# Attention scores from 16-bit pairs of turned heads in layer 0, and more buffers for raw weights

## The chip, the cores and the metric

The kernel runs on one core of one Trainium2 chip. The metric is the device time of one execution in microseconds (us). The kernel before takes 1107.42 us, the median of three runs (1106.44 to 1108.69).

A core has five engines, each with an instruction queue that it works off in order: TensorE (PE in the profile; its weight loads are listed apart as PEld), VectorE (DVE), ScalarE (ACT), GpSimd (POOL) and SyncE (SP). SP computes nothing here and only issues DMA transfers: loads of weights from HBM, and the DMA transposes that turn probability tiles. Tiles lie in SBUF. Matmul results lie in PSUM.

## The reference, cut to what matters

Two layers of a trunk run on 512 latent and 256 context tokens of width 1024. In each layer one input projection feeds two attentions: A, a neighbourhood attention of 8 heads, and B, a grouped-query attention of 8 query heads over 2 key heads, each head 64 wide. The change touches how q and k of B get from the projection to the scores.

```python
qb = _rope_2d(_rmsnorm(hs(b_q, GQA_Q_HEADS), q_norm_b), pos_row, pos_col)
kb = _rope_2d(_rmsnorm(hs(b_k, GQA_KV_HEADS), k_norm_b), pos_row, pos_col)
k_all = jnp.concatenate([ckb, kb], axis=1)
b_att = _gqa_latent(qb, k_all, v_all)
...
def _attend(q, k, v):
    s = jnp.einsum('bqkgd,btkd->bkgqt', q, k).astype(jnp.float32) * (HEAD_DIM ** -0.5)
    p = jax.nn.softmax(s, axis=-1).astype(v.dtype)
    return jnp.einsum('bkgqt,btkd->bqkgd', p, v)
...
o_a = (a_att * jax.nn.silu(a_z)) @ w_o_a
o_b = (b_att * jax.nn.silu(b_z)) @ w_o_b
merged = jax.nn.sigmoid(g_a) * o_a + jax.nn.sigmoid(g_b) * o_b
```

In layer 0 the context queries attend too (context keys only). Layer 1 needs latent queries alone.

## The kernel before

**Splitting.** To keep fp32 accuracy, a value is split into a high part (rounded) and a low part (the rest), and a product is a sum of matmuls over the parts. A weight tile arrives as `raw` (128x512, fp32); ACT casts it to `whi` (L405, L420), and DVE or POOL subtracts to get `wlo` (L408, L422). `raw_tile` gives these tiles out of three buffers in turn, so the DMA of a fourth waits in SP's queue until the subtraction of the first is done. There are eight `whi` and eight `wlo` buffers.

**Stages.** Each layer runs: projections of k, v and q of A; the neighbourhood attention (in layer 0 at about 150 to 300 us); projections of k, v and q of B (300 to 375 us), with rotary turns; the grouped-query attention (375 to 540 us); the merge. While an attention runs, PE also works through filler: pieces of the gate projections and of A's output projection, chunks of 24 matmuls (L435 to L437), placed between the heads. The two attentions each open a pool of tiles with `open_att` (tile width 512 for A, 768 for B).

**Order.** The program lists the operations; a scheduler that simulates the engines then sets each engine's order, so that moving one operation can reorder others. `behind` ties some to their place: the dot products of the modulation (L297: `rawb` times a broadcast row, on DVE) keep the order of the program on DVE.

**q and k of B.** `rope_heads` normalises and rotates a token tile; `turn` transposes it on PE into a PSUM tile `pst` (L529), and ACT copies that to `qb` (128 x 4 x 128, fp32) or `kb` (L543). After all tiles, `stage_k` makes, for each of the two key heads, `kh` (the high part on both halves of the partitions) and `kl` (the low part), with one DVE cast, two ACT casts and one POOL subtraction (L872 to L876). In the attention, `gq_first` calls `stage_q` for each of the eight heads: an ACT cast of 64x768 (L883) puts the high part of q on one half of the partitions, a DVE subtraction (L884) the low part on the other. So one matmul of the stacked q with `kh` and one with `kl` gives the score (L890, L891), 512 and 256 columns for each block of 128 queries.

**One head** of B in layer 0: for each of four query blocks PE writes a score tile `pss` (two buffers); DVE takes the row maxima (L1161); ACT takes the exponential and its sum (L1162), after which PE may use the buffer again; ACT rounds to 16 bits (`h`, L841), DVE or POOL subtracts the low part (L842), and SP issues the DMA transpose (L846). Then the context queries: L903 (maxima), L905 (a scalar added to them) on DVE, L909 (exponential) on ACT. The values of the head before follow: PE turns the reciprocals `r` (L851 on DVE, L853 on PE), multiplies the transposed probabilities (L1178, L1179; L925 for the context), ACT and DVE collect the result (`ho`, L828, L829), and POOL multiplies it into `zb` (L833). Once, `prepare` splits A's gated output into `gah` (ACT) and `gal` (POOL, four subtractions of 128x768, L672).

Of the kernel before, what the change touches and what calls it, by code (L numbers as in the profile page):

```python
# [28 lines left out]
NP_GQ = (2, 4)  # L29
NH_GQ = (3, 4)  # L30
# [4 lines left out]
P_UP = 2.0 ** 14  # L35
SPLIT_POOL = (1, 3)
# [36 lines left out]
def hybrid_kernel(es: ExitStack, tc, x, ctx, cvec, w_ada, w_ada0, small, gvec, w_in, w_o_a, w_o_b, w_out,  # L73
# [56 lines left out]
    cd = drp.tile([16, 128], F32, name="cd")  # L130
    gs = [drp.tile([128, 4, NTOK], F32, name=f"gs{c}") for c in range(4)]
# [40 lines left out]

    def raw_tile():
        return wp.tile([128, 512], F32, tag="raw", name=nm("raw"), bufs=3)
# [12 lines left out]
    G.memset(ehalf, -0.5)  # L187
# [39 lines left out]


# [295 lines left out]
    def turn(y, npair, dst, t, perm, g):  # L524
# [5 lines left out]
        if perm and t in (0, 3):  # L530

            src = pt.rearrange("p (j s n) -> p j s n", j=npair, s=2)
            d = dst[:, :, 0:512].rearrange("p j (s n) -> p j s n", n=64)
            if t == 0:
                d = d[:, :, 0:3:2, :]
            else:
                src, d = src[:, :, ::-1, :], d[:, :, 1:8:6, :]
        else:
            c0 = 128 * t + (64 if perm and t < 4 else 0)
            src = pt.rearrange("p (j n) -> p j n", j=npair)  # L540
            d = dst[:, :, c0:c0 + 128]
        if g is None:
            S.copy(d, src)  # L543
        else:
            S.activation(d, src, AF.Copy, scale=g)
# [49 lines left out]
    def layer(l, hx, nxt, start):  # L595
# [114 lines left out]
        kav = big("ka").rearrange("p (j n) -> p j n", j=4)  # L710
        if first:
# [7 lines left out]
            def evac_ak(ts):  # L719
# [9 lines left out]
                for i, t in enumerate(ts):  # L729
                    mul_heads(ys[t], ys[t], ss[:, 8 * i:8 * i + 8], 8)  # L730
                    to_channels(ys[t], 4, kav, t, False, gk)
# [3 lines left out]
        else:  # L735
# [3 lines left out]
            for t in range(6):  # L739
                tok_proj(w, 512, a_hx, t, evac_na(kav, False, gk, 4))  # L740
# [19 lines left out]
        w = load_w(W, C_AV, 512, KT, mix_lo)  # L760
        for t in range(6):
            tok_proj(w, 512, a_hx, t, evac_va)
            if first:
# [6 lines left out]
        qav = big("qa").rearrange("p (j n) -> p j n", j=4)  # L770
        w = load_w(W, C_AQ, 512, KT, mix_lo, own=hp["p"])
        za = big("za")
# [6 lines left out]
        for t in range(qt):  # L779
            tok_proj(w, 512, a_hx, t, evac_na(qav, True, gq, YB if first else 4))  # L780
# [10 lines left out]
        if True:  # L791
# [68 lines left out]
            def k_tile(e, zero):  # L860
                kh = att["p"].tile([128, 768], F32R, tag=f"kh{e}", name=nm("kh"), bufs=1)
                kl = att["p"].tile([128, 768], F32R, tag=f"kl{e}", name=nm("kl"), bufs=1)
                if zero:
                    V.tensor_scalar(rows(kl, 1 - e).rearrange("p (a b) -> p a b", b=128),
                                    rows(ident, 1 - e).unsqueeze(1).to_broadcast([64, 6, 128]),
# [664 lines left out]
```

## Time and profile before

| what | us |
|---|---|
| median of three runs (lowest, highest) | 1107.42 (1106.44, 1108.69) |
| profiled execution, its time | 1111.07 |
| span in that execution, first to last instruction | 1109.3 |
| PE busy in the span | 1075.5 |
| DVE busy | 767.4 |
| ACT busy | 617.1 |
| POOL busy | 473.1 |
| mean granted TensorE clock | 0.991 |

Busy time counts instructions in flight. Matmuls are pipelined, so that a row of the timeline shows a matmul of 0.4 us where the next one starts 0.23 us later; the step from start to start is what a matmul costs. "Idle before" in brackets is the time that an engine stood still ahead of an instruction, and the name behind the arrow is what ended the wait. PEclk is the share of full TensorE clock that was granted. The prediction shows the rows.

### The profile page before, as it was taken

Reading aid. Unit: us, or ns where it says so; the run is one execution under the profiler, and the core shown is the slowest. Engines: PE = TensorE matmul, PEld = TensorE weight load, DVE = VectorE, ACT = ScalarE, POOL = GpSimd, SP = SyncE. Lnnn points to the kernel's source line nnn. Section 1 sums busy time; section 2 is a strip of 40 time slices with the busy share of each in tenths; the row PEclk is TensorE's granted clock in tenths of the full one; section 3 lists DMA queues with packets and bytes.
Section 4 is the critical chain, followed back from the end, with each engine's and each line's share of the span. In section 5 each row is a group of like instructions: output and inputs, shape, how many; then the busy total and the mean of one; then the engine's idle time right before and its main releaser. Section 6 shows DMA issues by size and latency. Waiting matters only on the chain. (4 is left out here: it accounts for less than half of the span.)

```text
span 1109.3 us, 16937 instructions
## 1 busy us (share of the span) xinstructions
PE 1075.5 (97%) x5672; PEld 879.1 (79%) x5672; DVE 767.4 (69%) x1600; ACT 617.1 (56%) x1236; POOL 473.1 (43%) x397
## 2 busy tenths in 40 slices
PE   8999999999999989989999999999999999999998
PEld 5688888788888868767788878888877888777677
DVE  4667889975377487766777785366997665677473
ACT  6454279776433566765330275444899446786430
POOL 1054235555257154463621354232355472564531
PEclk9999999999999999998999999999999999999999
DMA  9455324554543379789633542453565536879642
GB/s 370 146 171 153 90 68 111 128 138 120 169 131 127 100 184 215 166 228 228 213 101 124 157 147 78 140 163 101 134 149 130 156 107 171 199 229 239 188 152 77
DMA packets 236000, 171.79 MB, mean 155 GB/s; under 512 B 160140, under 2 KB 201864, under 8 KB 234248
## 3 DMA queue, kind: packets, MB, share of 16 engines
q1 hardware_dynamic: 228576, 156.31, 51.6%
q0 software_dynamic: 2368, 7.87, 2.1%
q10 hardware_dynamic: 4968, 6.53, 1.8%
q8 instruction: 45, 0.74, 0.3%
q14 instruction: 43, 0.35, 0.1%
HBM read 115.58 MB, written 17.32 MB: 120 GB/s over the span
## 5 line engine op out<-in xcount | busy, mean ns | idle before, releaser
L842 POOL TENSOR_TENSOR h<-p,h 128x256 f16<-128x256 f32 (+2 forms) x104 | 113.6, 1101 | 160.0 <-ACT h L841 117.7
L422 POOL TENSOR_TENSOR wlo<-raw,whi 128x512 fp32r<-128x512 f32 x70 | 98.0, 1406 | 131.6 <-ACT whi L420 98.7
L435 PE MATMUL psf<-hx,whi 128*128 128x512 f32 (+1 forms) x360 | 138.2, 384 | 2.2 <-DVE zt L627 1.2
L436 PE MATMUL psf<-hx,whi 128*128 128x512 f32 (+1 forms) x360 | 136.1, 378 | 0.0
L437 PE MATMUL psf<-hx,wlo 128*128 128x512 f32 (+1 forms) x360 | 136.1, 378 | 0.0
L435 PE MATMUL psx<-whi,hx 128*128 128x512 f32 (+1 forms) x328 | 121.0, 372 | 0.0
L437 PE MATMUL psx<-whi,hx 128*128 128x512 f32 (+1 forms) x328 | 120.0, 367 | 0.0
L420 ACT CAST whi<-raw 128x512 fp32r<-128x512 f32 x136 | 83.2, 620 | 65.5 <-DMA raw<-in_w_in_dram 46.9
L436 PE MATMUL psx<-wlo,hx 128*128 128x512 f32 (+1 forms) x328 | 119.6, 366 | 0.0
L408 POOL TENSOR_TENSOR wlo<-raw,whi 128x512 fp32r<-128x512 f32 x40 | 59.8, 1499 | 117.7 <-ACT whi L405 74.6
L405 ACT CAST whi<-raw 128x512 fp32r<-128x512 f32 x88 | 54.3, 623 | 96.7 <-PE psx L437 34.2
L508 POOL TENSOR_TENSOR ss<-ss,ehalf 128x8 f32<-128x8 f32 (+2 forms) x40 | 63.6, 1593 | 77.2 <-DVE ss L505 72.2
L841 ACT CAST h<-p 128x256 f16<-128x256 f32 (+2 forms) x136 | 81.7, 616 | 5.3 <-DMA ht<-h 1.3
L422 DVE TENSOR_TENSOR wlo<-raw,whi 128x512 fp32r<-128x512 f32 x66 | 65.3, 992 | 25.9 <-ACT whi L420 24.3
L1161 DVE CUSTOM_DVE_ANT_0 p<-pss,vb 128x768 f32<-128x768 f32 x64 | 60.2, 953 | 31.0 <-PE pss L891 28.9
L1162 ACT ACTIVATE p<-pss,mx 128x768 f32<-128x768 f32 x64 | 57.6, 901 | 41.1 <-DVE mx L1161 40.4
L435 PEld LDWEIGHTS psf<-hx,whi 128*128 128x128 f32 x360 | 68.3, 190 | 14.9 <-ACT zt L625 1.9
L437 PEld LDWEIGHTS psf<-hx,wlo 128*128 128x128 f32 x360 | 68.2, 190 | 12.0
L436 PEld LDWEIGHTS psf<-hx,whi 128*128 128x128 f32 x360 | 68.3, 190 | 10.9
L437 PEld LDWEIGHTS psx<-whi,hx 128*128 128x128 f32 x328 | 61.9, 189 | 10.2
L436 PEld LDWEIGHTS psx<-wlo,hx 128*128 128x128 f32 x328 | 62.0, 189 | 9.5
L435 PEld LDWEIGHTS psx<-whi,hx 128*128 128x128 f32 x328 | 61.8, 189 | 9.1 <-issue 0.2
(338 smaller groups left out, 2984.7 us busy)
## 6 DMA issues: line engine op xcount, KB each, us to landing
raw<-in_w_in_dram SPq DMA_DIRECT2D x168, 256.0 KB, 3.0
rawb<-in_w_ada_dram SPq DMA_DIRECT2D x48, 256.0 KB, 2.8
raw<-in_w_out_dram SPq DMA_DIRECT2D x32, 256.0 KB, 2.9
tg<-gs SPq DMA_DIRECT2D x4, 1536.0 KB, 9.9
rawx<-in_w_ada_dram SPq DMA_DIRECT2D x4, 1024.0 KB, 10.3
rawy<-in_w_ada_dram SPq DMA_DIRECT2D x4, 1024.0 KB, 10.3
gs<-zt ACTq DMA_DIRECT2D x16, 256.0 KB, 2.6
raw<-in_w_o_a_dram SPq DMA_DIRECT2D x16, 256.0 KB, 3.1
```

The costliest lines, as they stand in the source:

```text
L405: S.copy(hi[:, :n], raw[:, :n])
L408: e.tensor_tensor(lo[:, :n], raw[:, :n], F(hi[:, :n]), ALU.subtract)
L420: S.copy(hi, raw)
L422: lo_eng(i).tensor_tensor(lo, raw, F(hi), ALU.subtract)
L435: T.matmul(ps, lhs[0], rhs[0], start=first, stop=False)
L436: T.matmul(ps, lhs[0], rhs[1], start=False, stop=False)
L437: T.matmul(ps, lhs[1], rhs[0], start=False, stop=last)
L508: G.tensor_tensor(ss, ss, ehalf[:, :n], ALU.pow)
L841: S.copy(h[:, 0], p[:, :n])
L842: eng.tensor_tensor(h[:, 1], p[:, :n], h[:, 0], ALU.subtract)
L1161: V.tensor_tensor_reduce(p, pss, lift, -1.0, 3e38, ALU.add, ALU.min, mx[:, 0:1])
L1162: S.activation(p, pss, AF.Exp, bias=mx[:, 0:1], accum_out=r[:, i:i + 1])
```

## The change

**Pairs in layer 0's grouped-query attention** (`GQ_PAIRS = (True, False)`). `turn` no longer copies the transposed tile as fp32. It writes fp16 pairs straight from PSUM: for q, ACT casts each half of the partitions (64 x 4 x 128) to the high part on its own half, and DVE subtracts the low part into the other half, so that `qb` holds the stacked q of every head, and `split_q` (the old `stage_q`) is not called. For k, one ACT cast and one DVE subtraction of 128x128 for each of six tiles, and then four DVE copies of 64x1536 (fp16) put each key head on both halves. To fit fp16, the norm gains are scaled by factors from their largest entries (`head_scales`, a few small operations at the stage's start), and the scores are scaled back by `gq_ndq` in L1161's place and `gq_dq` in the exponentials. The 160 score matmuls of this stage (64 of 512 columns, 96 of 256) take fp16 operands instead of fp32r.

**More raw buffers** (`MORE_RAW`). While an attention is open, every second `raw` tile comes from a second set: of one buffer in layer 0's neighbourhood attention and two in layer 1's, of three in layer 0's grouped-query attention, and none in layer 1's. The number of DMA transfers stays the same.

The same pairs for the neighbourhood attention are in the code and switched off (`NA_PAIRS`), so that none of their lines runs. Of the diff, what runs:

```diff
+MORE_RAW = ((1,2),(3,0))
+NA_PAIRS = (False, False)
+GQ_PAIRS = (True, False)
...
+H_UP = 2.0 ** 11
...
+    more_raw = {"p": None, "n": 0}
     def raw_tile():
-        return wp.tile([128, 512], F32, tag="raw", name=nm("raw"), bufs=3)
+        n = 3
+        if more_raw["p"] is not None:
+            more_raw["n"] += 1
+            if more_raw["n"] % 2 == 0:
+                return more_raw["p"]()
+        return wp.tile([128, 512], F32, tag="raw", name=nm("raw"), bufs=n)
...
-    G.memset(ehalf, -0.5)
+    G.memset(ehalf[:, 0:24], -0.5)
...
+    def head_scales(rows, inv, up):
+        S.activation(rows, rows, AF.Abs)
+        V.tensor_reduce(inv, rows, AX, ALU.max)
+        V.tensor_scalar(inv, inv, G_MIN, 1.0 / H_UP, ALU.max, ALU.mult)
+        V.reciprocal(up, inv)
...
+        def pair(hi, lo, x, g):
+            if g is None:
+                S.copy(hi, x)
+                todo.append(lambda: V.tensor_tensor(lo, x, hi, ALU.subtract))
...
+        kind, a, b = dst
+        for n0, n1, c0 in cuts:
+            x = pt.rearrange("p (j n) -> p j n", j=npair)[:, :, n0:n1]
+            da, db = [d[:, :, c0:c0 + n1 - n0] for d in (a, b)]
+            if kind == "k":
+                pair(da, db, x, g)
+                continue
+            for e, d in enumerate((da, db)):
+                own, other = slice(64 * e, 64 * e + 64), slice(64 - 64 * e, 128 - 64 * e)
+                pair(d[own], d[other], x[own], None if g is None else g[own])
+        run(todo, len(todo))
...
+            def stage_k(src, j, e, to, eng):
+                for half in range(2):
+                    eng(rows(to, half), rows(src, e)[:, :, j, :])
+            def q_pair(src, e, j):
+                return src[:, e, j, :]
...
+                pool, n_raw = att["p"], MORE_RAW[width == 768][l]
+                if n_raw:
+                    more_raw["p"] = lambda: pool.tile([128, 512], F32, tag="rawp", name=nm("raw"), bufs=n_raw)
+                st.callback(lambda: more_raw.update(p=None))
...
+                S.copy(g_abs, gbc)
+                head_scales(g_abs, g_inv, g_up)
+                V.tensor_scalar(gbc[:, 0, :], gbc[:, 0, :], g_up[:, 0:1], None, ALU.mult)
+                V.tensor_scalar(gbc[:, 1, :], gbc[:, 1, :], g_up[:, 1:2], 8.0, ALU.mult, ALU.mult)
+                V.tensor_tensor(gq_dq, g_inv[:, 0:1], g_inv[:, 1:2], ALU.mult)
+                V.tensor_scalar(gq_ndq, gq_dq, -1.0, None, ALU.mult)
...
-                    V.tensor_tensor_reduce(p, pss, lift, -1.0, 3e38, ALU.add, ALU.min, mx[:, 0:1])
-                    S.activation(p, pss, AF.Exp, bias=mx[:, 0:1], accum_out=r[:, i:i + 1])
+                    V.tensor_tensor_reduce(p, pss, lift, gq_ndq if gq_pairs else -1.0, 3e38, ALU.add, ALU.min, mx[:, 0:1])
+                    S.activation(p, pss, AF.Exp, bias=mx[:, 0:1], scale=gq_dq if gq_pairs else 1.0,
+                                 accum_out=r[:, i:i + 1])
...
-                q = stage_q(qbv[:, h // 2, :], h % 2)
+                kh, kl = gkt[h // 4][:2]
+                q = q_pair(qbv, h % 2, h // 2) if gq_pairs else split_q(qbv[:, h // 2, :], h % 2)
```

**Three places of the order.** Row by row: the line in the program, the operation, output<-inputs with buffer numbers, and the output's shape. In the program with the change the line of an operation is another: L297 is now L333, L422 L458, L829 L911, L842 L924, L851 L933, L854 L936, L903 L992, L905 L995, L1161 L1290, L417 L453, L846 L928, L953 L1051, L955 L1053.

First, DVE in the second head of layer 0's grouped-query attention, from the result of the head before (`ho`) to the first score of the next head. Before:

```order
L829 TENSOR_TENSOR ho_4525<-pst_4512,ho_4525 64x512
L903 TENSOR_REDUCE mx_4494<-pss_4489 128x2
L842 TENSOR_TENSOR h_4467<-p_4463,h_4467 128x768
L297 ISA rawb_4455,asum<-rawb_4455,vb_3419 128x512
L297 ISA asum 128x1
L851 RECIPROCAL r_868_4427<-r_868_4427 128x4
L905 TENSOR_SCALAR mx_4494<-mx_4494 128x2
L884 TENSOR_TENSOR qs_4932<-qb_3734,qs_4932 64x768
L829 TENSOR_TENSOR ho_4538<-psv_4529,ho_4538 64x256
```

With the change:

```order
L924 TENSOR_TENSOR h_4493<-p_4489,h_4493 128x768
L333 ISA rawb_4481,asum<-rawb_4481,vb_3419 128x512
L333 ISA asum 128x1
L911 TENSOR_TENSOR ho_4551<-pst_4538,ho_4551 64x512
L992 TENSOR_REDUCE mx_4520<-pss_4515 128x2
L933 RECIPROCAL r_866_4453<-r_866_4453 128x4
L995 TENSOR_SCALAR mx_4520<-mx_4520,vb_3419 128x2
L1290 ISA p_4711,mx_4712<-pss_4706,vb_3419 128x768
```

The subtraction for `h` and the dot product on `rawb`, which stood behind `ho` and ahead of the reciprocals of `r`, now stand ahead of `ho`; the subtraction for `qs` is gone.

Second, DVE two heads later, between the maxima of the context queries and the scalar added to them. Before:

```order
L829 TENSOR_TENSOR ho_5047<-psv_5038,ho_5047 64x256
L903 TENSOR_REDUCE mx_5003<-pss_4998 128x2
L884 TENSOR_TENSOR qs_5364<-qb_3734,qs_5364 64x768
L851 RECIPROCAL r_975_4936<-r_975_4936 128x4
L905 TENSOR_SCALAR mx_5003<-mx_5003 128x2
```

With the change:

```order
L992 TENSOR_REDUCE mx_5023<-pss_5018 128x2
L911 TENSOR_TENSOR ho_5067<-psv_5058,ho_5067 64x256
L933 RECIPROCAL r_971_4956<-r_971_4956 128x4
L995 TENSOR_SCALAR mx_5023<-mx_5023,vb_3419 128x2
L933 RECIPROCAL r_5027<-r_5027 128x2
```

The subtraction for `qs` has left the gap between the two, and the small `ho` (64x256) has come into it.

Third, SP's queue at the start of layer 0's neighbourhood attention, where the loads of filler weights (`raw`) stand between those of the position bias (`bint`, `bedg`) and the first transposes. Before:

```order
L953 DMA bint_1469<-in_bias_int_dram 128x256
L955 DMA bedg_1470<-in_bias_edge_dram 64x128 x2
L417 DMA raw_1645<-in_w_in_dram 128x2x256
L417 DMA raw_2025<-in_w_in_dram 128x2x256
L955 DMA bedg_1470<-in_bias_edge_dram 64x128 x2
L417 DMA raw_2031<-in_w_in_dram 128x2x256
L417 DMA raw_2037<-in_w_in_dram 128x2x256
L846 DMA_TRANSPOSE ht_1475<-h_1504 128x4x64 x2
L846 DMA_TRANSPOSE ht_1475<-h_1520 128x4x128
```

With the change:

```order
L1051 DMA bint_1473<-in_bias_int_dram 128x256
L1053 DMA bedg_1474<-in_bias_edge_dram 64x128 x2
L453 DMA raw_1637<-in_w_in_dram 128x2x256
L453 DMA raw_2041<-in_w_in_dram 128x2x256
L453 DMA raw_1649<-in_w_in_dram 128x2x256
L1053 DMA bedg_1474<-in_bias_edge_dram 64x128 x2
L453 DMA raw_2302<-in_w_in_dram 128x2x256
L453 DMA raw_2035<-in_w_in_dram 128x2x256
L928 DMA_TRANSPOSE ht_1479<-h_1508 128x4x64 x2
L928 DMA_TRANSPOSE ht_1479<-h_1524 128x4x128
```

One load more stands ahead of the first transposes, and the loads no longer go in the order of their numbers: those from the three old buffers run ahead of those from the one new buffer.

More of the change, by code (lines that the diff above doesn't have):

```diff
@@ L130, in hybrid_kernel @@
     cd = drp.tile([16, 128], F32, name="cd")
+    b_int = [drp.tile([8, 128, 256], F32, name=f"b_int{i}") for i in range(2)]
+    b_edge = [drp.tile([8, 128, 128], F32, name=f"b_edge{i}") for i in range(2)]
     gs = [drp.tile([128, 4, NTOK], F32, name=f"gs{c}") for c in range(4)]
@@ new lines, in turn @@
+        todo = []
+        if not isinstance(dst, tuple):
+            if perm and t in (0, 3):
+                x = pt.rearrange("p (j s n) -> p j s n", j=npair, s=2)
+                d = dst[:, :, 0:512].rearrange("p j (s n) -> p j s n", n=64)
+                if t == 0:
+                    d = d[:, :, 0:3:2, :]
+                else:
+                    x, d = x[:, :, ::-1, :], d[:, :, 1:8:6, :]
+            else:
+                x = pt.rearrange("p (j n) -> p j n", j=npair)
+                d = dst[:, :, cuts[0][2]:cuts[0][2] + 128]
+            if g is None:
+                S.copy(d, x)
+            else:
+                S.activation(d, x, AF.Copy, scale=g)
+            return
@@ L1034, in pipeline @@
                 run(fill, len(fill))
[L1036 removed]
+            akt = None if na_pairs else [k_tile(e) for e in range(2)]
             def na_first(h):
                 j, e = h // 2, h % 2
[L1040 to L1042 removed]
+                if na_pairs:
+                    kk = att["p"].tile([128, 2, 768], F16, tag="kk", name=nm("kk"), bufs=3)
+                    kh, kl = kk[:, 0], kk[:, 1]
+                    stage_k(kav, j, e, kk, V.tensor_copy)
+                    q = q_pair(qav, e, j)
+                else:
+                    kh, kl = akt[e]
+                    split_k(kav[:, j, :], e, kh, kl, False)
+                    q = split_q(qav[:, j, :], e)
                 st = na_scores(h, q, kh, kl)
```

144 lines of the change are left out of this document (94 added, 50 removed).

## The prediction

> **What bounds the kernel now.** I read the page's busy times first, then a table by stages, then PE's waits in the worst stage, then the timeline around the two longest of them. The page:
>
> ```profile
> span 1109.3 us, 16937 instructions
> PE 1075.5 (97%) x5672; PEld 879.1 (79%) x5672; DVE 767.4 (69%) x1600; ACT 617.1 (56%) x1236; POOL 473.1 (43%) x397
> ```
>
> PE has work in flight for 97% of the span, so only three things can shorten the kernel: cheaper matmuls, fewer idle gaps of PE, or a fuller clock. The table by stages (columns: window, its length, then busy time and count of PE, PEld, DVE, ACT, POOL, granted clock, DMA share, GB/s) tells where the gaps are:
>
> ```profile
> 150.00:300.00 150.00, 146.69 (x898) 125.21 (x897) 111.37 (x301) 109.63 (x247) 71.99 (x76) 1.00 0.51 129
> 300.00:375.00 75.00, 75.00 (x435) 65.48 (x435) 48.46 (x98) 29.72 (x60) 36.29 (x28) 1.00 0.40 129
> 375.00:540.00 165.00, 153.14 (x845) 123.38 (x844) 116.43 (x206) 104.58 (x203) 79.69 (x54) 0.96 0.78 193
> 920.00:1050.00 130.00, 126.53 (x595) 95.77 (x594) 83.93 (x134) 86.95 (x155) 67.19 (x45) 1.00 0.84 211
> ```
>
> Layer 0's grouped-query attention (375 to 540) has 11.9 us without a matmul, and it is the only one of these with a lower clock. Its twin in layer 1 (920 to 1050) misses 3.5, layer 0's neighbourhood attention 3.3, the projections of q and k (300 to 375) nothing. In windows of 10 us the clock falls twice:
>
> ```profile
> 405.00:415.00 10.00, 7.14 (x39) 6.07 (x40) 9.94 (x13) 4.22 (x10) 7.33 (x5) 0.79 0.38 107
> 415.00:425.00 10.00, 10.00 (x43) 7.36 (x42) 5.48 (x14) 5.82 (x10) 2.52 (x2) 0.87 1.15 235
> 495.00:505.00 10.00, 6.58 (x28) 5.48 (x27) 6.70 (x10) 3.90 (x7) 7.91 (x6) 0.72 1.05 342
> 505.00:515.00 10.00, 9.49 (x51) 7.78 (x49) 5.43 (x12) 4.18 (x9) 2.24 (x3) 0.93 1.00 244
> ```
>
> The missing clock is 2.1 + 1.3 = 3.4 us the first time and 2.8 + 0.7 = 3.5 the second. So the stage holds 11.9 + 6.9 = 18.8 us that are not matmuls at full rate, and that is the most that smoother running there can give. The largest waits of PE, on its timeline:
>
> ```profile
> 411.53 0.69 PE L853 MATMUL pst<-ident,r 128*128 128x128 f32 x2 [2.86 <-DVE mx L905]
> 452.64 0.50 PE L890 MATMUL pss<-gk,qs 128*128 128x512 f32 x1 [1.31 <-ACT p L909]
> 500.22 0.79 PE L890 MATMUL pss<-gk,qs 128*128 128x512 f32 x1 [2.71 <-ACT p L1162]
> ```
>
> Each drop of the clock goes with one of the two long ones. Both begin with a DVE instruction that took several times its usual length while POOL was at work:
>
> ```profile
> 406.77 4.61 DVE L297 CUSTOM_DVE_ANT_0 rawb<-rawb,vb 128x512 f32<-128x512 f32 x1
> 405.46 2.55 POOL L833 TENSOR_TENSOR zb<-zb,ho 64x512 f32<-64x512 f32 x1 [4.01 <-DVE ho L829]
> 407.98 1.63 POOL L842 TENSOR_TENSOR h<-p,h 128x768 f16<-128x768 f32 x1
> 409.58 1.25 POOL L422 TENSOR_TENSOR wlo<-raw,whi 128x512 fp32r<-128x512 f32 x1
> 493.94 3.60 DVE L842 TENSOR_TENSOR h<-p,h 128x768 f16<-128x768 f32 x1 [0.32 <-ACT h L841]
> 489.54 7.18 POOL L672 TENSOR_TENSOR gal<-za,gah 128x768 fp32r<-128x768 f32 x4
> ```
>
> The dot product on `rawb` that starts at 406.77 ends at 411.38, 0.55 us after POOL's row of three is through (409.58 + 1.25). The reciprocals of `r` stood behind it on DVE, and PE waited for them. The second time `h` is held until POOL is through with `gal`, and the maxima, the exponential and PE's score buffer behind it come late.
>
> **The change part by part.**
>
> *The work that moves.* From the attention go six q subtractions on DVE and six casts on ACT; two of each were done before 375 us. Into the projection stage come operations for which the trace has near rows only:
>
> ```profile
> L884 DVE TENSOR_TENSOR qs<-qb,qs 64x768 fp32r<-64x768 f32 x6 | 7.4, 1227 | 0.7 <-ACT qs L883 0.5
> L883 ACT CAST qs<-qb 64x768 fp32r<-64x768 f32 x6 | 5.0, 828 | 0.3 <-PE pst L853 0.3
> L829 DVE TENSOR_TENSOR ho<-pst,ho 64x512 f32<-64x512 f32 x8 | 5.5, 687 | 5.0 <-ACT ho L828 5.0
> L591 DVE TENSOR_TENSOR rr<-rr,ry 128x128 f32<-128x128 f32 x4 | 1.2, 288 | 1.2 <-POOL ry L588 1.1
> L872 DVE CAST gk<-kb 64x768 fp32r<-64x768 f32 x2 | 1.1, 549 | 0.0
> L543 ACT COPY qb<-pst 128x512 f32<-128x512 f32 x6 | 3.5, 584 | 5.3 <-PE pst L529 5.1
> ```
>
> DVE gets 12 subtractions of 64x512 from PSUM (12 x 0.687 = 8.2), six of 128x128 (6 x 0.288 = 1.7), four copies of 64x1536 for two casts of 64x768 (between 4 x 0.549 and twice that, less 1.1: 1.1 to 3.3), and loses two q subtractions (about 1 each): 9.0 to 11.2 us net, with the head scales some eight tiny operations more. ACT's six copies become twelve casts, about +3.5, against fewer k and q casts. At most 48.5 + 11 + 1 = 61 of 75 us of DVE are then busy, under a PE that is never idle there. I cost this move at nothing. PE covers it: in the new order 59 matmuls stand between the last turned tile and the first score, over 7 us at 0.12 each, while the last tile needs two casts and two subtractions, 2 x 0.58 + 2 x 0.69 = 2.5 us. With that cover gone it would cost 2.5.
>
> *Cheaper score matmuls.* Steps from start to start:
>
> ```profile
> 486.70 0.40 PE L890 MATMUL pss<-gk,qs 128*128 128x512 f32 x1
> 486.93 0.40 PE L891 MATMUL pss<-gk,qs 128*128 128x512 f32 x1
> 487.17 0.28 PE L890 MATMUL pss<-gk,qs 128*128 128x256 f32 x1
> 487.29 0.28 PE L891 MATMUL pss<-gk,qs 128*128 128x256 f32 x1
> 490.08 0.38 PE L1178 MATMUL pst<-ht,vb 128*128 128x512 f16 x1 [0.93 <-DVE zb L854]
> 492.45 0.38 PE L1179 MATMUL pst<-ht,vb 128*128 128x512 f16 x1
> 403.10 0.61 PE L925 MATMUL psv<-vb 128*128 128x256 f16 x4
> ```
>
> The 512-column score takes 0.235 (487.17 less 486.70, halved); the fp16 value matmuls of 512 columns, twelve between the two rows, step by 2.37 / 11 = 0.215. For 256 columns it is 0.12 against (0.61 - 0.28) / 3 = 0.11. So 64 x 0.02 + 96 x 0.01 = 2.2 us at most; nothing, if it is the score's place and not its type that sets the step. I take 1.5, nearer the fp16 rows.
>
> *The stall at 411.* In the new order `h` and the dot product stand ahead of `ho` on DVE. POOL's `zb` of 405.46 waits for that `ho`, so the row of three POOL operations can no longer be under way when the dot product starts; and the reciprocals of `r` now follow `ho` and a reduction from PSUM. The 2.86 us wait goes, and with it the drop of the clock, 3.4: 6.3 us. If the same collision only moves to POOL's `h` that now stands ahead of `zb`, DVE loses at most that operation's 1.63 us, and the gain shrinks by it.
>
> [...] Here the clock fell by waits of 2.86 and 2.71, so I go by the trace.
>
> *The wait at 452.* These rows carry it:
>
> ```profile
> 448.29 0.67 DVE L903 TENSOR_REDUCE mx<-pss 128x2 f32<-128x512 f32 x1
> 448.99 1.00 DVE L884 TENSOR_TENSOR qs<-qb,qs 64x768 fp32r<-64x768 f32 x1
> 450.11 1.42 DVE L905 TENSOR_SCALAR mx<-mx 128x2 f32<-128x2 f32 x1
> 449.39 2.12 POOL L842 TENSOR_TENSOR h<-p,h 128x768 f16<-128x768 f32 x1 [0.22 <-ACT h L841]
> L829 DVE TENSOR_TENSOR ho<-psv,ho 64x256 f32<-64x256 f32 x7 | 2.9, 420 | 3.9 <-ACT ho L828 3.7
> ```
>
> The tiny L905 is held until POOL's `h` ends (449.39 + 2.12 = 451.51). Without the q subtraction it would come sooner, but the small `ho` that now stands there (0.42 us) puts it at about 449.4 (448.29 + 0.67 + 0.42), just when POOL's `h` starts. The gain is 1.3 or nothing; I take nothing.
>
> *More raw buffers.* In the grouped-query stage none of PE's waits ends on a raw load, so a deeper prefetch saves nothing by itself: 0. In layer 0's neighbourhood attention half of the loads now go through one buffer, so each of these waits for the load two before it, where it waited for the load three before. Bounds: no cost, as PE's largest waits there are not for weights, and the slower rival below.
>
> ```profile
> PE psf L435 <- DVE zt L627: 1.2, 1, 1.2
> PE psv L925 <- DVE ho L832: 1.1, 1, 1.1
> ```
>
> *New waits.* DVE and ACT together have 12.4 us less to do in the attention's 165 (7.4 + 5.0), but the order on every engine is new. Between nothing and one more episode like 411's (6.3). I take one wait of the stage's usual size, +1.3.
>
> **Sum:** -1.5 - 6.3 + 1.3 = -6.5 us. The profiled execution took 1111.07 us (the span and 1.8 around it), 0.3% above the median of 1107.42; the terms are differences, so I set them against the median: 1107.4 - 6.5 = **1101 us**.
>
> **The rivals.**
>
> *Both episodes go.* The relieved DVE reaches `h` before POOL's four `gal` start, so that the 2.71 wait at 500 and its 3.5 of clock go too, and no new wait comes: 1101 - 6.2 - 1.3 = 1093.5. For it: the stage loses 12 us of DVE and ACT work. Against it: the four `gal` are untouched and still stand one behind another, 7.18 us in which an `h` on DVE can be caught.
>
> *The stall only moves.* Another two-input operation of DVE meets another row of POOL work, as POOL's `h` and `zb` come in every head. The score's 1.5 is kept, and 1.3 of new wait comes: 1107. Against it: the stage in layer 1 runs the same mix on the same engines with 3.5 us idle and a full clock. [...]
>
> *Slower: the single new buffer blocks SP's queue.*
>
> ```profile
> SPq L417 <- POOL wlo L422: 14.2, 3, 12.5
> ```
>
> One raw load already held SP for 12.5 us in the neighbourhood attention, waiting for a POOL subtraction. With loads out of turn (the third load of the new order belongs to a later chunk), such a wait can come with transposes behind it that PE needs. PE has one chunk of filler to bridge it, 24 x 0.23 = 5.5 us, so 12.5 - 5.5 = 7.0 us of wait and a drop of the clock, 3.4: 1101 + 10.4 = 1111. It decides from a hold of over 5.5 us. Against it: the 12.5 of before cost PE nothing.
>
> **How the numbers follow.** Chances: forecast 0.48 (1097 to 1105), both go 0.15, it only moves 0.22, the slower rival or another new episode 0.15. About 0.2%, 2.2 us, is what a measurement of this kernel can tell from no change. Faster: 0.46 of the forecast, 0.15 and 0.03, together 0.64. Same: 0.02, 0.14 and 0.01, 0.17. Slower: 0.05 of a stall that moves and grows, and 0.14, 0.19. The range leaves out about a tenth on each side: from 1092, just below the case that both go, to 1111.
>
> **What would show it.** Right: no DVE operation over 3 us ahead of the second head's reciprocals, one drop of the clock in this stage instead of two, PE idle there near 9 us, fp16 scores of 512 columns stepping by 0.215. Wrong: two or more drops of the clock still in the stage; PE idle between 300 and 375 (the cover fails); waits of PE for `ht` or for `wlo` in the neighbourhood attentions, where SP stood long on a raw load.

## The result, and the profile after

The changed kernel takes 1114.53 us (median of 6 runs, 1112.86 to 1115.50) against 1108.31 for the kernel before beside it: a ratio of 1.0053, 95% interval 1.0037 to 1.0070. It is 6 us slower, where 6.5 less had been forecast. The page of the profile after (span, then busy time of each engine):

```profile
span 1111.9 us, 16941 instructions
PE 1076.6 (97%) x5672; PEld 866.9 (78%) x5672; DVE 770.3 (69%) x1618; ACT 615.0 (55%) x1232; POOL 466.3 (42%) x395
```

The table by stages of the kernel after, with the columns of the prediction (window, its length, busy time and count of PE, PEld, DVE, ACT and POOL, granted clock, DMA share, GB/s):

```profile
300.00:375.00 75.00, 74.63 (x431) 64.85 (x430) 57.03 (x124) 28.04 (x59) 33.68 (x26) 1.00 0.45 139
375.00:540.00 165.00, 153.00 (x860) 113.55 (x860) 115.02 (x205) 105.22 (x199) 82.91 (x57) 0.97 0.80 189
610.00:690.00 80.00, 76.24 (x357) 61.01 (x356) 58.75 (x109) 37.13 (x84) 35.19 (x39) 1.00 0.39 124
775.00:850.00 75.00, 72.72 (x369) 58.68 (x369) 71.78 (x200) 69.09 (x153) 39.45 (x41) 0.98 0.62 143
```

The same table of the kernel before, for the two stages of which the prediction shows no row:

```profile
610.00:690.00 80.00, 78.08 (x371) 64.12 (x370) 58.92 (x110) 39.42 (x87) 37.34 (x39) 1.00 0.40 125
775.00:850.00 75.00, 73.38 (x381) 58.87 (x380) 69.76 (x197) 68.46 (x152) 35.42 (x40) 1.00 0.58 139
```

Two stages that the prediction never priced are worse: layer 0's merge with layer 1's first projections (610 to 690) has 3.8 us without a matmul instead of 1.9 (a second profile of the kernel before, shown further down, has 0.1 there), and layer 1's neighbourhood attention (775 to 850) has PE a little less busy and a lower clock. Waits of PE on its timeline in these stages, of the kernel after:

```profile
454.15 0.96 PE L1019 MATMUL psv<-ct,vb 128*128 128x256 f16 x4 [2.76 <-DMA ct<-h]
496.29 0.58 PE L471 MATMUL psf<-gah,whi 128*128 128x256 f32 x1 [2.86 <-DVE tg L770]
638.27 0.98 PE L379 MATMUL pst<-ident,y 128*128 128x128 f32 x7 [1.63 <-DVE y L370]
651.78 0.50 PE L472 MATMUL psx<-wlo,hx 128*128 128x512 f32 x1 [0.86 <-DVE wlo L444]
653.84 0.33 PE L379 MATMUL pst<-ident,y 128*128 128x128 f32 x1 [0.62 <-ACT half L382]
658.26 0.50 PE L472 MATMUL psx<-wlo,hx 128*128 128x512 f32 x1 [0.45 <-DVE wlo L444]
812.68 0.79 PE L1076 MATMUL pss<-kh,qs 128*128 128x512 f32 x1 [2.28 <-DVE mx L1079]
```

The stall at 411 is gone. The one at 500 is there still, a wait for the context transposes at 454 has grown, and those near 652 and at 812 are new. (The one at 638 is not part of the change: the kernel before has 1.68 there in its first profile and none in its second.) In windows of 10 us the kernel after loses clock around three of them:

```profile
405.00:415.00 10.00, 9.30 (x57) 7.51 (x55) 8.67 (x19) 7.80 (x17) 6.39 (x5) 1.00 0.80 186
450.00:460.00 10.00, 7.24 (x33) 5.17 (x32) 7.28 (x13) 7.62 (x14) 4.79 (x3) 0.83 1.03 225
490.00:500.00 10.00, 6.88 (x30) 4.86 (x29) 6.70 (x9) 5.39 (x10) 6.81 (x5) 0.76 0.80 269
805.00:815.00 10.00, 7.72 (x41) 5.77 (x40) 9.80 (x22) 8.86 (x21) 6.08 (x6) 0.88 0.57 128
815.00:825.00 10.00, 10.00 (x53) 8.12 (x52) 9.78 (x29) 9.24 (x21) 5.17 (x5) 0.95 0.55 109
```

To see where time goes when stages shift, I laid the profiles side by side at equal PE work: every matmul counted with its usual step (0.226 us for 512 columns, 0.119 for 256), and the time in the span at which so much work was issued. "Again" is a second profile of the kernel before, "held" the experiment pairs_gq_old_merge below.

```
PE work  before   again   after    held   place
 360      384.9   384.8   385.5   385.5   layer 0's grouped-query attention begins
 520      570.4   568.5   567.2   565.3   it has ended
 580      631.3   629.0   627.9   625.7   merge
 640      696.6   692.9   696.8   689.1   layer 1's first projections
 740      800.5   796.7   800.7   793.0   inside layer 1's neighbourhood attention
 760      821.5   818.7   825.9   813.7   the same
1020     1098.9  1096.1  1101.5  1088.8   near the end
```

From 360 to 520 the kernel after gains 3.8 us on the first profile of before and 2.0 on the second; from 580 to 640 it loses 3.6 and 5.0, from 740 to 760 it loses 4.2 and 3.2. The operations of the merge are unchanged. Their order is not: the scheduler, which simulates the engines, gave 610 to 690 another order once the attention ahead of it differed. The same measure over all sixteen profiles of this case sets that order apart: from 550 to 640 of PE work the eleven whose merge goes in the old order take 93.8 to 96.3 us, the five with the new order 98.6 to 99.5.

### The profile page after: what moved, and what is told of

It is laid out like the page before. It is cut to its first block, busy times and chain, and to the rows that moved or that the text cites. A ratio compares the mean times of both kernels' runs of the same rounds, so it can differ in the third digit from the quotient of the medians.

```text
span 1111.9 us, 16941 instructions
## 1 busy us (share of the span) xinstructions
PE 1076.6 (97%) x5672; PEld 866.9 (78%) x5672; DVE 770.3 (69%) x1618; ACT 615.0 (55%) x1232; POOL 466.3 (42%) x395
## 4 chain that ended last, share of the span: by engine, by line
PE 62%; DVE 13%; issue 8%; DMA 7%; ACT 5%; POOL 3%; SPq 1%; POOLq 0%; DVEq 0%; ACTq 0%
PE psx L473 9%; PE psx L472 9%; PE psx L471 9%; PE psf L471 7%; PE psf L472 7%; PE psf L473 7%; DMA ht<-h 2%; DMA raw<-in_w_in_dram 2%; PE pss L979 1%; DMA rawb<-in_w_ada_dram 1%; PE pss L980 1%; DVE wlo L458 1%; PE pst L565 1%; DVE p L1079 1%; PE pst L1308 1%
## 5 line engine op out<-in xcount | busy, mean ns | idle before, releaser
L924 POOL TENSOR_TENSOR h<-p,h 128x256 f16<-128x256 f32 (+2 forms) x104 | 115.4, 1117 | 173.9 <-ACT h L923 118.5
L458 POOL TENSOR_TENSOR wlo<-raw,whi 128x512 fp32r<-128x512 f32 x70 | 97.3, 1396 | 116.6 <-ACT whi L456 82.2
L444 POOL TENSOR_TENSOR wlo<-raw,whi 128x512 fp32r<-128x512 f32 x40 | 54.1, 1356 | 121.6 <-ACT whi L441 82.8
L544 POOL TENSOR_TENSOR ss<-ss,ehalf 128x8 f32<-128x8 f32 (+2 forms) x40 | 66.1, 1655 | 90.6 <-DVE ss L541 85.8
L458 DVE TENSOR_TENSOR wlo<-raw,whi 128x512 fp32r<-128x512 f32 x66 | 67.3, 1024 | 34.1 <-ACT whi L456 32.8
L1290 DVE CUSTOM_DVE_ANT_0 p<-pss,vb 128x768 f32<-128x768 f32 x64 | 62.3, 984 | 36.4 <-PE pss L980 31.7
L471 PE MATMUL psx<-hx,whi 128*128 128x256 f32 (+1 forms) x208 | 68.7, 330 | 0.0
```

The costliest lines, as they stand in the source:

```text
L444: e.tensor_tensor(lo[:, :n], raw[:, :n], F(hi[:, :n]), ALU.subtract)
L458: lo_eng(i).tensor_tensor(lo, raw, F(hi), ALU.subtract)
L471: T.matmul(ps, lhs[0], rhs[0], start=first, stop=False)
L544: G.tensor_tensor(ss, ss, ehalf[:, :n], ALU.pow)
L924: eng.tensor_tensor(h[:, 1], p[:, :n], h[:, 0], ALU.subtract)
L1290: V.tensor_tensor_reduce(p, pss, lift, gq_ndq if gq_pairs else -1.0, 3e38, ALU.add, ALU.min, mx[:, 0:1])
```

## The experiments

All ratios are to the kernel before on the same chip, with 95% intervals.

**Which part costs?** Four kernels with parts of the change, made by two lines:

```diff
-MORE_RAW = ((1,2),(3,0))
-GQ_PAIRS = (True, False)
+MORE_RAW, GQ_PAIRS = ((0,0),(0,0)), (True, False)    # pairs_alone
+MORE_RAW, GQ_PAIRS = ((0,0),(3,0)), (True, False)    # pairs_gqbuf
+MORE_RAW, GQ_PAIRS = ((1,0),(3,0)), (True, False)    # no_na1_buf
+MORE_RAW, GQ_PAIRS = ((1,2),(0,0)), (False, False)   # na_bufs_alone
```

> Pairs in layer 0's grouped-query attention, no extra raw buffer anywhere; the order outside of that stage and the projections ahead of it is that of before. Theory P (the pairs do what was forecast and the loss comes from the two extra raw buffers of layer 1's neighbourhood attention): 1101 to 1106 us, faster than before by 2 to 7. Theory Q (the pairs themselves cost, by a new wait for the context's transposes in the stage): 1110 or more. Theory R (the loss is layer 0's single extra buffer): as theory P here.

> Pairs and the three extra raw buffers in layer 0's grouped-query attention, none in the neighbourhood attentions. Theory P: 1101 to 1106 us. Theory Q: 1110 to 1114. Theory R: 1101 to 1106. Against the run with the pairs alone it tells what the three buffers are worth; theories P and R expect within 2 us of it.

> The change without the two extra raw buffers of layer 1's neighbourhood attention: layer 1 has the order of before, layer 0 that of the change. Theory P: 1102 to 1107 us, some 7 to 12 below the whole change, and no half clock and no wait of 2 us in layer 1's neighbourhood attention. Theory Q: 1112 to 1115, as the whole change. Theory R: 1110 to 1114.

> Only the extra raw buffers of the two neighbourhood attentions (one and two), no pairs, none in the grouped-query attentions. Theory P: 1111 to 1115 us, slower than before by 3 to 7, with the wait of about 2.3 us and the half clock in layer 1's neighbourhood attention as in the whole change. Theory Q: 1107 to 1110, as before. Theory R: 1110 to 1113, and the time is lost in layer 0's neighbourhood attention.

Measured: pairs_alone 1113.31 us (1.0048, 1.0029 to 1.0066), pairs_gqbuf 1110.87 (1.0016, 1.0001 to 1.0031), no_na1_buf 1110.69 (1.0016, 1.0000 to 1.0032), na_bufs_alone 1113.77 (1.0037, 1.0020 to 1.0053). No theory holds for all four: the pairs lose without any buffer, as theory Q has it, and the buffers of the neighbourhood attentions lose without the pairs, as theory P has it. The single buffer of layer 0's neighbourhood attention changes nothing that the times can tell (1.0016 with and without it); in the traces its stage, 100 to 280 of PE work, takes 191.5 to 191.7 us in the four kernels that have it and 190.3 to 190.7 in the others. The slower rival, some 10 us through SP's queue, is out. Layer 1's two buffers cost some 4 us (1113.77 against 1109.05 of before, and the whole change against no_na1_buf). The pairs alone cost 4 to 5, although their attention is shorter, and the three buffers of the grouped-query attention win half of that back or a little more.

**Is it the new order of the merge?** In these kernels the instructions from the merge's start to layer 1's first projections are chained on each engine in an order taken from another kernel; no wait for another engine is added.

```diff
+    for order in HELD.values():        # one list of instructions for each engine
+        last = None
...
+                if last:
+                    tc.add_manual_dep(i, last, mybir.DependencyInfo(
+                        mybir.DependencyClass.NoSync, mybir.DependencyReason.DATA), reason="held order")
+                last = i.name
```

> Turned pairs and three raw buffers in layer 0's grouped-query attention, and from the start of the merge to layer 1's first projections the instructions of every engine held in the order that they have in the kernel before. Theory M (the attention keeps its gain, and the scheduler's new order of the merge and of layer 1's first tiles gives it back): about 3 us below the 1110.87 of the same kernel in its own order, so 1107 to 1108.5, and PE's waits for wlo and half near 650 us are gone. Theory T (the profile of before was one of its slow executions, so that there is less to gain than it shows): 1110 to 1111.5, whatever the order of the merge.

> The kernel before, with the merge and layer 1's first projections held in the order that the pairs bring; no pairs, no further buffer. Theory M: 2.5 to 4 us slower than before, with the waits of 0.86, 0.62 and 0.45 us near 650 us that the kernels with pairs show. Theory T: the time of before within 1 us.

> The whole change, with the merge and layer 1's first projections held in the order of before. Theory M (layer 0's merge in its new order takes back what the attention gains, and layer 1's neighbourhood attention adds 4 us through its two buffers): 1114.5 less 7, so 1107 to 1109, that is 4 us above the 1103.9 of the same kernel without buffers in the neighbourhood attentions. Rival (the held order helps only where nothing else is changed): 1111 or more.

> Turned pairs alone, no further raw buffer anywhere, the merge held in the order of before. If the pairs by themselves do what the prediction says (its sum without the buffers, -6.5): 1102 to 1105. If the three buffers of the grouped-query attention carry part of the gain, as the 2.4 us between pairs_alone and pairs_gqbuf let suppose: 1106 to 1107.

| kernel | new order of the merge | before's order |
|---|---|---|
| before | 1.0014 (1.0003 to 1.0024) | 1 |
| pairs | 1.0048 (1.0029 to 1.0066) | 1.0016 (0.9997 to 1.0035) |
| pairs, three buffers | 1.0016 (1.0001 to 1.0031) | **0.9957** (0.9943 to 0.9970) |
| whole change | 1.0053 (1.0037 to 1.0070) | 1.0017 (1.0001 to 1.0033) |

In medians the right column is 1110.19 for the pairs, 1103.92 with the three buffers, 1110.98 for the whole change; before with the new order took 1111.29. In every row the new order costs: 0.14% of the kernel before, 0.32 to 0.59% of the others, or 1.6 to 6.5 us. The expectations missed in size. before_new_merge lost 1.6 us, between what theory M (2.5 to 4) and theory T (within 1) gave; pairs_gq_old_merge came out 3 us under theory M; after_old_merge, at 1110.98, lies above M's 1107 to 1109 and close to its rival's 1111; the pairs alone fit neither expectation, as even with the old order they gain nothing. The table by stages of before_new_merge, 610 to 690, and its waits there (the line numbers of the experiments differ from those after by a few, here by 9):

```profile
610.00:690.00 80.00, 77.13 (x356) 60.92 (x355) 56.83 (x109) 37.11 (x85) 34.77 (x38) 1.00 0.38 123
```

```profile
651.09 0.50 PE L481 MATMUL psx<-wlo,hx 128*128 128x512 f32 x1 [0.88 <-DVE wlo L453]
653.14 0.66 PE L388 MATMUL pst<-ident,y 128*128 128x128 f32 x4 [0.63 <-ACT half L391]
```

and the stage of pairs_gq_old_merge, where PE never stops (the second profile of the kernel before comes close, with 79.86 of 80, so the 1.9 us of its first profile do not belong to the old order):

```profile
610.00:690.00 80.00, 80.00 (x386) 66.44 (x385) 58.20 (x106) 42.24 (x92) 39.48 (x41) 1.00 0.41 130
```

So the waits of 0.86, 0.62 and 0.45 belong to the order, with pairs or without. The timeline of the kernel before shows how ACT takes turns there between the tiles of `hx` (`half`) and the weights (`whi`):

```profile
647.52 1.54 ACT L346 ACTIVATE half<-pst,modc 128x128 f32<-128x128 f32 x4
648.89 0.68 ACT L405 CAST whi<-raw 128x512 fp32r<-128x512 f32 x1
649.64 1.06 ACT L330 ACTIVATE full<-xt 128x1024 f32<-128x1024 f32 x1
```

and that of the kernel after, DVE and POOL beside ACT, how three casts go together:

```profile
646.85 1.70 ACT L441 CAST whi<-raw 128x512 fp32r<-128x512 f32 x3
647.58 2.99 POOL L444 TENSOR_TENSOR wlo<-raw,whi 128x512 fp32r<-128x512 f32 x2 [2.41 <-ACT whi L441]
649.35 1.77 DVE L1384 TENSOR_TENSOR xt<-xt,t 128x512 f32<-128x512 f32 x1
651.04 0.68 DVE L444 TENSOR_TENSOR wlo<-raw,whi 128x512 fp32r<-128x512 f32 x1
651.24 1.06 ACT L366 ACTIVATE full<-xt 128x1024 f32<-128x1024 f32 x1 [2.69 <-DVE xt L1384]
```

Three casts release two subtractions on POOL in a row; the addition into `xt` on DVE (usually 0.68) lasts 1.77 us and ends 0.55 us after them (651.12 against 650.57), and `wlo` behind it, for which PE waits, and `full` on ACT come late. What those waits sum to, 1.9 us, is less than the order costs with the pairs; the rest I could not place in one row. In the traces the stage loses as much without pairs: by the measure above before_new_merge takes 99.5 us there, the kernel before 96.3 and 94.4.

**What do layer 1's two buffers do?** Two kernels with these buffers alone: one holds PE and DVE of layer 1 in the order of before; the other sends all loads of that attention through four buffers in turn, which leaves PE, DVE and POOL in the order that the change's two buffers give.

```diff
             more_raw["n"] += 1
-            if more_raw["n"] % 2 == 0:
-                return more_raw["p"]()
+            return more_raw["p"]()         # na1_four_in_turn, MORE_RAW = ((0,4),(0,0))
```

> The kernel before with two more raw buffers in layer 1's neighbourhood attention alone, PE and DVE of layer 1 held in the order of before; ACT, POOL and SP follow the buffers. Theory O (the two buffers cost by the new order, in which a DVE subtraction and a DVE cast meet POOL at 806 to 811 us and PE then waits 2 us and loses the clock): 1109 to 1110.5, no wait over 1.5 us near 811. Theory B (they cost by the loads themselves, which come out of turn through two sets of buffers): 1113 or more, with the waits elsewhere.

> The kernel before; in layer 1's neighbourhood attention all raw loads go through four buffers of its own, one after the other, where the change sends every second one through two of its own. PE, DVE and POOL then have the same order as with the change's two buffers. Theory O (the order costs: a subtraction on DVE and a cast meet POOL near 806 to 811 us, PE waits 2 us and loses the clock): 1112 to 1114, with that wait. Theory B (it is the loads out of turn that cost): the time of before within 1.5 us.

The first took 1116.97 (1.0071, 1.0059 to 1.0084) and can't be read as meant: ACT was free to put its casts of the weights last, DVE's held order stood waiting for them, and PE with it:

```profile
770.17 0.80 PE L477 MATMUL psf<-hx,whi 128*128 128x512 f32 x1 [7.54 <-DVE za L696]
```

What follows comes from the stretch behind that stall: up to 847 us, in which the other kernels with these buffers have their wait, it has none over 0.5 us, and from 710 to 900 of PE work it takes 201.5 us. The eleven profiles without these buffers take 201.7 to 202.9 there, the four with the buffers and the new order 205.3 to 206.1. The second took 1112.47 (1.0035, 1.0020 to 1.0049), as much as two buffers out of turn, with the wait where theory O has it:

```profile
809.25 0.50 PE L1074 MATMUL pss<-kh,qs 128*128 128x512 f32 x1 [2.08 <-DVE r L875]
```

So the loads out of turn do not matter, and with PE and DVE in the old order the buffers cost that stretch nothing: it is their order. The timeline of the kernel after, DVE and POOL, shows the place:

```profile
806.97 1.55 POOL L915 TENSOR_TENSOR za<-za,ho 64x512 f32<-64x512 f32 x1 [3.60 <-DVE ho L914]
807.35 1.74 DVE L458 TENSOR_TENSOR wlo<-raw,whi 128x512 fp32r<-128x512 f32 x1
810.22 1.26 POOL L458 TENSOR_TENSOR wlo<-raw,whi 128x512 fp32r<-128x512 f32 x1
810.25 1.65 DVE L961 CAST kh<-ka 64x768 fp32r<-64x768 f32 x1
811.93 0.69 DVE L1079 CUSTOM_DVE_ANT_0 p<-pss,bint 128x512 f32<-128x512 f32 x1
```

With more buffers a weight comes earlier, and its subtraction is put between two heads on DVE, where it takes 1.74 us beside POOL's `za` (0.69 in four of its other seven rows from 775 to 850 us); then the cast of `kh` takes 1.65 us beside POOL's own `wlo` (0.54 to 0.58 in its other rows there), and the maxima that free PE's score buffer come late, and PE waits 2.28 us; the clock then misses 1.2 + 0.5 us (0.88 and 0.95 above). The wait comes with the buffers, the drop of the clock not each time: na_bufs_alone has a wait of 2.03 there and a full clock (1.00 from 805 to 815), where its expectation had half.

**Is the profile of before typical?**

> A second profile of the kernel before (its instructions in the same order). If the two drops of the clock at 411 and 500 us belong to it, both are there again and layer 0's grouped-query attention misses 6 to 7 us of clock, in a time of 1107 to 1112. Theory T: one of them is gone and the attention is 3 us or more shorter than the 150.8 us between its first and its last score that the first profile has.

It took 1107.56 us. The two waits are there, 2.79 and 2.71:

```profile
410.40 0.90 PE L935 MATMUL pst<-ident,r 128*128 128x128 f32 x3 [2.79 <-DVE mx L999]
498.24 0.50 PE L979 MATMUL pss<-gk,qs 128*128 128x512 f32 x1 [2.71 <-ACT p L1291]
```

but each costs half the clock that it cost in the first profile, 1.7 us instead of 3.4:

```profile
405.00:415.00 10.00, 7.21 (x38) 6.06 (x37) 9.87 (x14) 4.17 (x11) 7.54 (x5) 0.83 0.49 133
415.00:425.00 10.00, 10.00 (x57) 7.78 (x57) 6.44 (x15) 6.85 (x12) 1.65 (x1) 1.00 1.09 248
495.00:505.00 10.00, 7.29 (x33) 6.31 (x33) 6.43 (x14) 5.51 (x10) 6.49 (x5) 0.83 1.07 289
```

Theory T is right by 1.7 us for each episode, not in its claim that one is gone. Four more kernels have this attention in the order of before (before_new_merge, na_bufs_alone and the two of layer 1's buffers), and in the profile of each both episodes cost 1.7: the 3.4 of the first profile is the exception, one of six.

**What takes the gain of the pairs when they stand alone?** In pairs_old_merge, the timelines of POOL, DVE and PE at 521 us:

```profile
521.26 1.65 POOL L933 TENSOR_TENSOR h<-p,h 128x768 f16<-128x768 f32 x1
521.96 3.42 DVE L1004 TENSOR_SCALAR mx<-mx,vb 128x2 f32<-128x2 f32 x1
522.88 2.47 POOL L467 TENSOR_TENSOR wlo<-raw,whi 128x512 fp32r<-128x512 f32 x2
525.89 0.79 PE L480 MATMUL psf<-gah,whi 128*128 128x512 f32 x1 [3.61 <-DVE tg L779]
```

The scaling of the context maxima, two numbers a partition, stands 3.42 us on DVE (to 525.38), until POOL is through with three operations (522.88 + 2.47 = 525.35), and PE waits 3.61 us behind it. In the kernel after it takes 0.19 to 0.23 us in four of the eight heads. Two kernels move it to ACT, every other instruction in its place:

```diff
-                    V.tensor_scalar(mx, mx, dq, P_LOG if late else 0.0, ALU.mult, ALU.add)
+                    S.activation(mx, mx, AF.Copy, bias=P_LOG if late else 0.0, scale=dq)
```

> The kernel of pairs_old_merge (1110.19 beside 1109.58 of before), with one operation of each head, the scaling of the context maxima mx (128x2), on ACT instead of DVE; every other instruction in the same order. If that operation, held by POOL's row h, wlo, wlo for 3.4 us at 522 us, is what ends PE's wait of 3.6 us for tg and halves the clock there, the wait falls under 1.5 us and the time by 3 to 6 us, to 1104 to 1107. If the next DVE instruction, the subtraction of wlo, is held by the same row for as long: 1109 to 1111, with the wait still there.

> The same edit on the kernel of pairs_gq_old_merge (1103.92; 0.9957 of before), where that operation took 1.3 us and PE's wait behind it was 1.5. If the three buffers gain mainly by drawing POOL's row apart ahead of that operation, little is left: 1102 to 1104 (0.994 to 0.996 of before). If they gain by something else: 1099 to 1101.

pairs_mx_on_act took 1108.94 (1.0001, 0.9990 to 1.0013). The wait fell to 0.51 us, but the time only by 1.7 of the 3 to 6 expected (1.0016 to 1.0001), which the intervals do not tell from nothing. POOL's row now holds the next one (3.29 us), and another wait of 3.2 has come; timelines of DVE, ACT and PE:

```profile
520.37 3.29 DVE L467 TENSOR_TENSOR wlo<-raw,whi 128x512 fp32r<-128x512 f32 x1
531.00 0.62 ACT L465 CAST whi<-raw 128x512 fp32r<-128x512 f32 x1 [2.83 <-DMA raw<-in_w_o_b_dram]
531.65 0.69 DVE L467 TENSOR_TENSOR wlo<-raw,whi 128x512 fp32r<-128x512 f32 x1 [4.80 <-ACT whi L465]
535.95 0.39 PE L480 MATMUL psf<-gah,whi 128*128 128x256 f32 x1 [3.20 <-DVE tg L779]
```

A late raw load holds ACT for 2.83 us, then `wlo` at the head of DVE's queue for 4.80, and behind it the `tg` for which PE waits 3.20. This is a way from a raw load to PE that no wait of PE names. ACT waits over 0.3 us for a raw load five times between 375 and 545 us in pairs_old_merge, 6.8 us in all, and once in pairs_gq_old_merge, but for 4.75. There pairs_gq_mx_on_act gained nothing (1104.28; 0.9961, 0.9945 to 0.9977): with three buffers the row at 521 cost little (the operation took 1.34 us and PE's wait behind it 1.52).

**The stall near 494 us.** `gal` on DVE instead of POOL, on the kernel of pairs_gq_old_merge:

```diff
-            hilo(za, gated["a"], range(4))
+            hilo(za, gated["a"], range(4), V if first else G)
```

> The kernel of pairs_gq_old_merge, with the four subtractions that make gal in layer 0 on DVE instead of POOL. If POOL's row of four (7.2 us) is what holds DVE's h and then PE for 2.9 us near 494 and the clock for 3.4, both go and nothing comes instead: 1098 to 1101. If DVE's own row of four (some 4 us) holds the maxima just as long: 1103 to 1106.

It took 1105.00 (0.9965, 0.9950 to 0.9980), no better than without the edit (0.9957). The wait of 2.86 became one of 1.25 and several of 0.5 to 1.6. That DVE's own row of four holds its queue instead is my estimate; no row here times it. In its profile the clock no longer drops there (1.00 from 490 to 510 us).

**How much of it is clock?** Each run has its span and its mean granted clock on record, and the span times one less the clock is the time that the clock took from it. One run's figure is rounded to about 1 us, so only means say something (standard error in brackets): 7.0 us (0.4) in the kernel before, 9.1 (0.8) in pairs_old_merge, 5.1 (0.8) in pairs_gq_old_merge, 6.8 (0.4) in pairs_mx_on_act, 3.4 (0.5) in gal_on_dve, 6.1 (0.4) in before_new_merge. So some 4 of the 6.5 us between the pairs with and without the three buffers are clock, and moving `mx` to ACT won clock and, as far as these means tell, nothing else. With `gal` on DVE the clock takes less, but the rest of the time grew by 2.5 us (1.0).

## Why the prediction was wrong

*Cheaper scores: right.* In the kernel after, the fp16 score of 512 columns steps by 0.215, as forecast:

```profile
490.93 0.38 PE L979 MATMUL pss<-gk,qb 128*128 128x512 f16 x1
491.14 0.38 PE L980 MATMUL pss<-gk,qb 128*128 128x512 f16 x1
491.36 0.27 PE L979 MATMUL pss<-gk,qb 128*128 128x256 f16 x1
```

In the median the 256-column score steps by 0.109 where it took 0.118, so the steps give 64 x 0.02 + 96 x 0.009 = 2.1 us against the 1.5 taken. No run shows this term as time by itself.

*The work that moves: right.* DVE is busy 57.0 of 75 us from 300 to 375 (at most 61 forecast), and PE idle for 0.4.

*The stall at 411: right in its place, too large in its size.* It went as forecast, by the order of `h` and `ho`: the dot product is through before POOL's row starts. The timelines of DVE and POOL after:

```profile
405.48 0.69 DVE L333 CUSTOM_DVE_ANT_0 rawb<-rawb,vb 128x512 f32<-128x512 f32 x1
406.78 1.66 POOL L924 TENSOR_TENSOR h<-p,h 128x768 f16<-128x768 f32 x1 [6.31 <-DVE ho L911]
```

Its clock, 3.4 us, came from one profile; five others show 1.7. So 4.5 us rather than 6.3.

*The wait at 452 and the new waits: too small.* The 1.31 went, and the wait behind it, for the context transposes, grew from 0.98 (at 458.62 in the kernel before) to 2.76 us and took 1.7 of clock: the step "new waits, +1.3" measured about 2.2 (2.76 + 1.7 - 1.31 - 0.98). Why it grew, no run shows. By the prediction's own signs the stage went both ways: no DVE operation over 3 us stands ahead of the second head's reciprocals, but the clock still drops twice (at 454 and 495 us), and PE is idle for 12.0 us instead of near 9. With 2.0 to 3.8 us gained where 6.5 was forecast, the attention ended between the forecast and the rival in which the stall only moves.

*More raw buffers, 0 in the grouped-query stage: wrong.* They gain 0.32% with the new order of the merge and 0.59% with the old one. "None of PE's waits ends on a raw load" was true of the kernel before and did not bear the conclusion: in pairs_mx_on_act a late load reached PE through the order of DVE (2.83 us on ACT, 4.80 on DVE, 3.20 on PE). That the gain runs this way is read from the traces, not tried by itself, and some 4 of the 6.5 us with the old order are clock (above).

*More raw buffers in the neighbourhood attentions: priced in the wrong layer.* I set a rival against layer 0's one buffer, which costs nothing that the times can tell, and gave layer 1's two no term; they cost 4 to 7 us (1.0053 against 1.0016 with the new order of the merge; 1.0017 against 0.9957 with the old, where layer 0's one buffer is in the difference too).

*The step that failed most* is one that the sum never wrote down: that the stages which the change does not edit keep their time. The prediction read the moved rows at three places and not in the merge, where the new order costs 0.32 to 0.59% of the kernels with pairs. The runs close the sum: the whole change is 5.9 us slower by its ratio; holding the merge takes off 4.0, leaving out the buffers of the neighbourhood attentions 6.6 more (each to about 2.5 us). With that order held and no buffers in the neighbourhood attentions, the kernel takes 0.9957 of before, 4.8 us less: 1.7 short of the -6.5 forecast. But that kernel has the gain of the three buffers in it, which I had at nothing; the pairs alone, with the order held, gave no gain that can be measured. So the agreement is partly luck.

What stays open is why the new order makes the kernel before only 0.14% slower, and the others by 0.32 to 0.59%, when the merge itself loses as much in its trace as in theirs (that before_new_merge loses 1.1 us less clock than the kernel before is one part of it), and how far the three buffers gain by the late loads alone.

## What to carry to other kernels

Where a scheduler sets the order, compare it before and after over the whole program, also in stages whose code is the same, and price every stage that differs; then hold those stages in their old order to see what the edit itself is worth. A buffer or an edit that frees an engine is paid for where the scheduler puts the freed work: in layer 1's neighbourhood attention a subtraction that came earlier landed beside POOL's work, took 1.74 us, and PE's wait behind that queue came to 2.28. Here holding the merge turned a loss of 0.2% into a gain of 0.4% (pairs_gq_old_merge, 1103.92 us), the lowest median found, though the two kernels built on it are too close to tell apart.

## What the runs showed of the hardware

PE's idle time of about the same length did not always cost the same clock. From 490 to 500 us PE is without a matmul for 3.1 us in pairs_gq_old_merge (6.89 of 10 busy) and for 2.9 in pairs_gq_mx_on_act (7.14); the first lost 3.4 us of clock (0.66) there, the second none (1.00). Of these two kernels in turn:

```profile
490.00:500.00 10.00, 6.89 (x24) 5.20 (x24) 7.58 (x11) 4.99 (x8) 5.76 (x5) 0.66 0.88 187
```

```profile
490.00:500.00 10.00, 7.14 (x40) 5.26 (x41) 8.73 (x14) 6.47 (x11) 5.40 (x4) 1.00 0.79 167
```

The losses come in lumps, 1.7 us (0.83 of a window of 10) or 3.4 (0.66): half clock for 3.41 or 6.83 us in the clock records of the first profile of the kernel before and of the kernel after. In both the starts of half clock lie a whole number of 3.413 us apart: 118, 26 and 178 times that in the kernel before, where the two in the attention are 88.75 us apart, and 12, 93 and 87 times in the kernel after. Waits of 2.08 (na1_four_in_turn, 0.83 from 805 to 815 us) to 2.86 us went with half clock, while neither the 2.9 us of idle time above nor the wait of 2.03 in na_bufs_alone did (1.00 each); why one does and another does not, no run shows. The same two waits of the kernel before cost 3.4 us of clock each in one profile and 1.7 in the other, so an estimate of a lost clock from one execution was off by a factor of two here.

In pairs_old_merge one DVE instruction on two numbers a partition (L1004) stood for 3.42 us, until three POOL operations in a row were through (`h` and two `wlo`, 521.26 to 525.35).
